# Moving VectorE's work behind a pointwise product: low weights one slot sooner, sums of y spread out, parts of the second half's y sooner

## The chip, the core and the metric

The kernel runs on one core of a Trainium2 chip. The core has a matrix engine (TensorE, PE in the profile), three engines for element-wise work (VectorE or DVE, ScalarE or ACT, GpSimd or POOL) and a queue engine (SyncE, SP) that issues most transfers. The metric is the device time of one execution in microseconds (us). Three runs of the kernel before gave 811.04, 811.59 and 811.87 us; their median is 811.59 us.

## What is computed

One decoder layer on 512 tokens and 2048 channels. After an RMS norm, one wide product makes seven pieces of 1024 columns: value, gate and output gate of a convolution module, q, k, v, and the gate of attention. The convolution half (mixer A) ends in a pointwise projection, the attention half (mixer B) in a gated mixture of three dilated patterns. Both halves meet in the output product.

```
u = silu(layer_norm(causal_depthwise_conv(a_val * sigmoid(a_glu))))
y_a = (u @ conv_pw_w + conv_pw_b) * silu(a_gate)
y_b = dilated_attention_mixture(rms(q), rms(k), v) * silu(b_gate)
out = x + concat(y_a, y_b) @ w_out
```

## The kernel before

Most products are exact to about float32 by being made of float16 pairs. A tile is scaled by a power of two, rounded to float16 (the high part, written by ACT), and the rest is kept as a second float16 tile (the low part, written by DVE as source times scale less high part). `tri` (line 447) then does three matmuls, lines 449, 450 and 451. The scale comes from `bound` (line 215): ACT sums the squares of each piece (`row_squares`, line 213, an ACTIVATE into `junk` with an accumulator), PE adds the columns of sums over partitions by a small matmul with ones (line 225), DVE reduces the result, POOL takes an inverse root (lines 227 and 191), and DVE rounds it to a power of two and inverts it.

Weights come in units of 4 x 128 rows by 512 columns. For a plain unit, `split_hi` (line 326, ACT, tile `wh`) and `split_lo` (line 334, DVE, tile `wl`) make the parts of the next unit while the current one is multiplied. A plain unit is 8 slots; a slot holds 6 matmuls of 512 columns.

All engines run in program order, and the program order is written by hand. `after(n, fn)` (line 143) puts a piece of work n slots ahead in a calendar; tables of numbers at lines 56 to 81 say how far. What is due in a slot is issued before the matmuls of that slot. An instruction that stands late in DVE's order therefore waits for all of DVE's work ahead of it, whatever its own inputs do.

The tail of the program runs as follows. One unit of the output product's group `wb` 0 takes the first half of y_b; then come the pointwise product `pw` (two groups of two units), one unit of `wb` 3 and one of `wc` 0 (they take parts of y_b), and last the four groups `wa` in `seven_products` (line 1097). These replace eight block products by seven, and so need sums of blocks of weights and of blocks of y:

- The evacuation of `pw` (line 929) multiplies by the gate of mixer A. It is the DVE instruction that writes `gate` or `ag` from `ps_l`, four for each group. `put_y` (line 683) has ACT square the result for the bound of all of y (`yab`), and after the second group's four pieces `y_sums` (line 708) forms the block sums: two subtractions at once (`ysum<-ag`, 128x256) and two dependent operations a slot later (`ysum<-gate,ysum`).
- `bound("yab", ...)` gives the scale `yas`. `y_parts` (line 782) then splits sixteen pieces of y (line 748 on ACT, line 749 on DVE).
- The second half of y_b (`b1`) has a scale of its own, `yb1s`. `b_parts` (line 764) splits its four pieces with `plain` (lines 761 and 762) for the unit `wc` 0, and its sums by `y_sums` and `block`. The first half (`b0`) is treated alike, earlier, from line 1393.
- Sums of weight blocks are made in place, partly by DVE and partly by accumulating transfers that POOL issues (line 1038). `both_scales` (line 1084) forms, on POOL, the scales of a `wa` group: `esc`, `nesc` and the joined scales `wjs` (lines 1093 and 1094), which ACT needs for the parts `wsc` and `wsd`.

Of the kernel before, what the change touches and what calls it, by code (L numbers as in the profile page):

```python
# [59 lines left out]
SHIFT_FROM = 3  # L60
SHIFT_STEP = 5
LN_STEPS = [4, 1, 2, 2, 4, 4, 1, 1]
B0_AT = -11
YB = [0, 1, 4, -2, -1, 2]
B_STEPS = [-5, 2, 19, 6]
B1_STEPS = [3, 12, 28, 6]
Y_STEPS = [3, 1]
IN_HI = [-5, -5, -5, -5, -5, -4, -4]
IN_ADD = {('s1', 0): -8, ('s1', 1): -7, ('s2', 0): -1, ('s2', 1): 1, ('s3', 0): 13, ('s3', 1): 11, ('s4', 0): 8, ('s4', 1): 9}
IN_OUT = [4, 8, 16, 9, 12, 16, 20, 24, 24, 25, 25, 27, 28, 29]  # L70
NORM_7 = {'q': [1, 5, 6, 8], 'k': [3, 7, 9, 10]}
NORM = {'q': [3, 8, 8, 10, 5], 'k': [3, 7, 9, 13, 5]}
NORM_K0 = [3, 1, 10, 11, 13, 2]
WA_ADD = [{'s1': (4,), 's4': (1,), 's2': (-2,), 's3': (-8,)}, {'s1': (8, 9, 14), 's4': (2, 3, 8), 's2': (-2, -1, 4), 's3': (-13, -12, -12)}, {'s1': (8, 9, 12), 's4': (2, 3, 8), 's2': (-2, -1, 4), 's3': (-16, -15, -16)}, {'s1': (5, 6), 's4': (0, 2), 's2': (-3, -2), 's3': (-16, -15)}]
WA_PARTS = [{'a11': (-29,), 'a22': (-27,), 'a12': (-1,), 's3': (1,), 's2': (4,), 's1': (7,), 's4': (9,)}, {'a11': (-8, -7, -3), 'a22': (-4, -3, 2), 'a12': (-2, 2, 5), 's3': (4, 5, 10), 's2': (8, 9, 14), 's1': (11, 12, 17), 's4': (15, 16, 21)}, {'a11': (-7, -7, -2), 'a22': (-4, -3, 2), 'a12': (-1, 0, 5), 's3': (4, 5, 10), 's2': (8, 9, 14), 's1': (11, 12, 17), 's4': (15, 16, 21)}, {'a11': (-5, -5), 'a22': (-4, -3), 'a12': (-2, -1), 's3': (0, 1), 's2': (4, 5), 's1': (7, 8), 's4': (10, 11)}]
WA_OUT = [1, 4, 1, 5, 5, 6, 6]
MEASURE = 16
# [1 line left out]
SPLIT_AT = [0, 3]  # L79
# [28 lines left out]
def layer(ctx: ExitStack, tc: tile.TileContext, xt, w1, w2, w3, g_in, conv_w, conv_b,  # L108
# [34 lines left out]
    def after(n, fn):  # L143

        calendar.setdefault(clock[0] + max(n, 1), []).append(fn)
# [180 lines left out]
    def split_hi(i):  # L326
        if i < n_plain:
            parts[i] = [part_pool.tile([P, KU, S], F16, name=n, tag="part") for n in ("wh", "wl")]
            A.activation(parts[i][0], raw[i], AF.Copy, scale=wscale[units[i][3:]][0])  # L329

    def of_next(i):
        return units[min(i + 4, len(units) - 1)][3:]

    def split_lo(i):
        if i < n_plain:
            wh, wl = parts[i]
            V.scalar_tensor_tensor(wl, raw.pop(i), wscale[units[i][3:]][0], wh, op0=OP.mult, op1=OP.subtract)
            load(i + RING)
            after(MEASURE_AT[of_next(i) not in SEVEN], lambda: measure(i + RING))
# [337 lines left out]
    yf = {"a": {}, "b0": {}, "b1": {}}  # L677
# [5 lines left out]
    def put_y(part, i, y):  # L683

        at = i + {"b0": 0, "a": 4, "b1": 12}[part]
        if not ysum:
            ysum.append(small.tile([P, 16], BF16, name="ysum", bufs=1))
        row_squares(y, ysum[0][:, at:at + 1], S, evac_scale(("pw", 0)) if part == "a" else 1.0)
        yf[part][i] = y
        if part != "a" and len(yf[part]) == 4:  # L690
            n = at - 3

            def done(s, v):
                scales["y" + part] = s, v
                if part == "b1":
                    b1_parts()

            after(YB[0], lambda: bound("y" + part, ysum[0][:, n:n + 4], done, TOP - 1, YB[1:3]))
        if part == "a" and i >= 4:
            after(1 + 4 * (i == 7), lambda: y_sums("", yf["a"], i - 4, i))  # L700
        summed.add(at)
        if len(summed) == 16:
            after(YB[3], lambda: bound("yab", ysum[0], y_parts, TOP - 1, YB[4:]))

# [3 lines left out]
    def y_sums(c, y, k, below):  # L708

        b11, b12 = (y[k][:, f:f + H] for f in (0, H))  # L710
        b21, b22 = (y[below][:, f:f + H] for f in (0, H))
        if not c and k < 2:
            t = att.tile([P, 2, S], F32, name="ysum2", tag="att")
            t12, t34 = t[:, 0], t[:, 1]
        else:
            t12, t34 = slot("ysum"), slot("ysum")
        t1, t2, t3, t4 = t12[:, :H], t12[:, H:], t34[:, :H], t34[:, H:]
        V.tensor_sub(t1, b11, b12)
        V.tensor_sub(t3, b12, b22)

        def rest():
            V.tensor_add(t2, b22, t1)
            V.tensor_sub(t4, b21, t2)

        after(1, rest)
        for name, t in (("b11", b11), ("b2", y[below]), ("t12", t12), ("t34", t34)):
            if name[0] == "t" or not c:
                yt[name + c, k] = t
# [35 lines left out]
    def b_parts(part):  # L764
        y = dict(yf[part])
        s = scales["y" + part][0]
        c = "d" if part == "b0" else "c"
        o = B_STEPS if part == "b0" else B1_STEPS
        for k in range(4):
# [12 lines left out]
    def y_parts(s, v):  # L782
# [6 lines left out]
        for name in ("b11", "t34", "b2", "t12"):  # L789
            for k in range(4):  # L790
                n += 1
                after(max(n - Y_STEPS[0], n // Y_STEPS[1]), lambda name=name, k=k: block(name, k, sa))

# [220 lines left out]
    def seven_parts(g):  # L1014
# [62 lines left out]
        for name, at in WA_PARTS[g].items():  # L1077
            for c, n in zip(kinds, at):
                plan += [(n, name + c, hi), (n + 1, name + c, lo)]
        adds = [(n, name + c, add) for name, at in WA_ADD[g].items() for c, n in zip(kinds, at)]  # L1080
        plan = [(n, lambda name=name, fn=fn: fn(name)) for n, name, fn in plan + adds]
# [310 lines left out]

    calendar.setdefault(8 * of_group["wb", 0][0] + B0_AT, []).append(b0_parts)
    for n, fn in seven_parts(0):
        if n < 0:
            calendar.setdefault(BEGIN[0] + n, []).append(fn)
    for i in range(n_plain):
        kind, g = group = units[i][3:]
        if group in SEVEN:
            if i == of_group[group][0]:  # L1400
                plan = ahead.pop(i) + later
                later = []
                n_next = i + 4
                if units[n_next][3:] in SEVEN:
                    ahead[n_next] = input_products(n_next)
                    plan += [(n + 28, fn) for n, fn in ahead[n_next] if n < 0]
                else:
                    plan = [(24, lambda: split_hi(n_next)), (25, lambda: split_lo(n_next))] + plan
                for n in range(28):
                    clock[0] = 8 * i + n + n // 7  # L1410
                    for fn in due_now():
                        fn()
                    first = [fn for k, fn in plan if k == n]
                    for fn in first[:]:
                        if fn.__name__ != "matmuls":
                            fn()
                    run_conv()
                    for fn in first:
                        if fn.__name__ == "matmuls":
                            fn()  # L1420
                later = [(n - 28, fn) for n, fn in plan if n >= 28]
                if units[n_next][3:] not in SEVEN:
                    for n, fn in later:
                        after(8 * n_next + n - clock[0], fn)
                    later = []
                if kind == "k":
                    attention(g)
            continue
        exact = i < n_exact
        if exact:  # L1430
            order = [(None, None)] * 8
        else:
            order = [(m, hf) for m in range(4) for hf in range(2)]
            extra = [[] for _ in range(8)]
            if i + 1 < len(units) and units[i + 1][3:] in SEVEN:
                ahead[i + 1] = input_products(i + 1)
                for n, fn in ahead[i + 1]:
                    if n < 0:
                        extra[max(n, -8)].append(fn)
            else:  # L1440
                extra[SPLIT_AT[0]].append(lambda: split_hi(i + 1))
                extra[SPLIT_AT[1]].append(lambda: split_lo(i + 1))
            if i + 1 < len(units) and units[i + 1][3] == "wb":
                for m in range(2):
                    extra[4 * m].append(lambda m=m: fetch_res(2 * units[i + 1][4] + m))
            if units[i + 1][3] in ("wb", "wc"):
                extra[3].append(lambda: evac_scale(units[i + 1][3:]))
            if units[i + 1][3:] == ("pw", 0) and kind != "pw":
                extra[3].append(pw_bias)
        if kind == "pw":  # L1450
            need = KU * units[i][2] + KU - 1
            while need not in u16:
                next(convolution)
        for n, (m, hf) in enumerate(order):
            clock[0] = 8 * i + n
            if exact:
                extra = {n: startup(clock[0])}
            due = due_now()
            for fn in extra[n] + due if exact or kind in ("wb", "wc") else due + extra[n]:
                fn()  # L1460
            run_conv()
            done = exact_matmuls(clock[0]) if exact else slot_matmuls(i, m, hf)
            if done:
                done()
        if kind == "k" and i == of_group[group][-1]:
            attention(g)
# [71 lines left out]
```

## Time and profile before

| what | value |
|---|---|
| median of three runs | 811.59 us (811.04 to 811.87) |
| the profiled execution | 811.37 us |
| span of its instructions | 809.6 us |
| granted clock of PE | 1.000 |
| busy DVE / ACT / POOL | 718.5 / 571.5 / 162.3 us |
| HBM read | 88.56 MB |

The profile was taken on one execution. Its times count from the first instruction; the 1.8 us between the span and the execution's own time lie outside the instructions. In a timeline a row gives start, duration, engine, line, operation, output and inputs, and in brackets how long the engine had been idle and what released it. DVE's instructions all have line 103, the helper that records them. A plain DVE instruction of 512 columns is shown with about 0.74 us and the next starts 0.66 us after it, so an engine's rows may overlap slightly. The profile prints the tiles `y16` as `y`.

### The profile page before, as it was taken

Reading aid. Unit: us, or ns where it says so; the run is one execution under the profiler, and the core shown is the slowest. Engines: PE = TensorE matmul, PEld = TensorE weight load, DVE = VectorE, ACT = ScalarE, POOL = GpSimd, SP = SyncE. Lnnn points to the kernel's source line nnn. Section 1 sums busy time; section 2 is a strip of 40 time slices with the busy share of each in tenths; the row PEclk is TensorE's granted clock in tenths of the full one; section 3 lists DMA queues with packets and bytes.
Section 4 is the critical chain, followed back from the end, with each engine's and each line's share of the span. In section 5 each row is a group of like instructions: output and inputs, shape, how many; then the busy total and the mean of one; then the engine's idle time right before and its main releaser. Section 6 shows DMA issues by size and latency. Waiting matters only on the chain.

```text
span 809.6 us, 13885 instructions
## 1 busy us (share of the span) xinstructions
PE 801.9 (99%) x5448; PEld 518.5 (64%) x5448; DVE 718.5 (89%) x1208; ACT 571.5 (71%) x800; POOL 162.3 (20%) x165
## 2 busy tenths in 40 slices
PE   9999999999999999999999999999999999999998
PEld 6887745888888854444444444444544444888887
DVE  6768899899999989999899999899699679998784
ACT  6667775677878697757849458496799868667530
POOL 0002021213535101104113010110230012423310
PEclk9999999999999999999999999999999999999999
DMA  9853253685979946352863825327282646898551
GB/s 339 337 232 104 105 145 98 123 261 94 299 160 272 224 150 169 105 147 82 175 170 102 182 94 157 117 66 165 95 199 75 165 161 157 208 223 233 106 117 53
DMA packets 88097, 130.87 MB, mean 162 GB/s; under 512 B 62688, under 2 KB 67040, under 8 KB 78816
## 3 DMA queue, kind: packets, MB, share of 16 engines
q1 hardware_dynamic: 80544, 107.37, 43.2%
q0 software_dynamic: 7200, 22.55, 15.5%
q8 instruction: 42, 0.69, 0.3%
q14 instruction: 23, 0.19, 0.1%
q10 hardware_dynamic: 288, 0.07, 0.0%
HBM read 88.56 MB, written 4.19 MB: 115 GB/s over the span
## 4 chain that ended last, share of the span: by engine, by line
PE 92%; DVE 5%; POOL 1%; ACT 1%; issue 1%; DMA 0%; SPq 0%; DVEq 0%; POOLq 0%; ACTq 0%
PE ps_l L449 24%; PE ps_l L450 24%; PE ps_l L451 24%; PE ps_l L978 11%; PE ps_s L824 2%; PE ps_o L865 2%; PE ps_s L449 2%; PE ps_s L451 2%; PE ps_s L450 2%; DVE res L103 1%; DVE y L103 1%; DVE ysum L103 1%; DVE ws L103 0%; POOL wf L1038 0%; DMA x<-xt_dram 0%
## 5 line engine op out<-in xcount | busy, mean ns | idle before, releaser
L103 DVE SCALAR_TENSOR_TENSOR cv<-u,cw,cv 128x511 f32<-128x511 f32 (+14 forms) x240 | 162.2, 727 | 2.7 <-ACT cv L614 2.7
L213 ACT ACTIVATE junk<-wf 128x2048 uint8<-128x2048 f32 x68 | 129.1, 1899 | 8.8 <-DMA wf<-w_dram 8.7
L449 PE MATMUL ps_l<-x,wh 128*128 128x512 f16 x320 | 121.3, 379 | 0.0
L451 PE MATMUL ps_l<-x,wl 128*128 128x512 f16 x320 | 121.3, 379 | 0.0
L450 PE MATMUL ps_l<-x,wh 128*128 128x512 f16 x320 | 121.3, 379 | 0.0
L103 DVE SCALAR_TENSOR_TENSOR ws<-wf,ws 128x1024 f16<-128x1024 f32 x84 | 107.2, 1278 | 8.0 <-ACT ws L1216 6.8
L329 ACT ACTIVATE wh<-wf,ws 128x2048 f16<-128x2048 f32 x39 | 77.7, 1993 | 25.5 <-PE ps_l L450 21.5
L103 DVE SCALAR_TENSOR_TENSOR wl<-wf,ws,wh 128x2048 f16<-128x2048 f32 x39 | 91.4, 2344 | 3.1 <-ACT wh L329 2.9
L449 PEld LDWEIGHTS <-wh 128*128 128x128 f16 x432 | 42.3, 98 | 54.1 <-issue 5.0
L451 PEld LDWEIGHTS <-wl 128*128 128x128 f16 x432 | 42.2, 98 | 52.0 <-issue 1.1
L450 PEld LDWEIGHTS <-wh 128*128 128x128 f16 x432 | 42.2, 98 | 48.4 <-issue 0.3
L449 PE MATMUL ps_l<-wh,x 128*128 128x512 f16 x192 | 72.8, 379 | 0.0
L451 PE MATMUL ps_l<-wh,x 128*128 128x512 f16 x192 | 72.8, 379 | 0.0
L450 PE MATMUL ps_l<-wl,x 128*128 128x512 f16 x192 | 72.8, 379 | 0.0
L978 PE MATMUL ps_l<-xr,wr 128*128 128x512 f32 x288 | 69.6, 397 | 0.2 <-ACT xr L367 0.2
L227 POOL TENSOR_SCALAR ws<-ws 128x1 f32<-128x1 f32 x20 | 18.7, 937 | 248.0 <-DVE ws L103 247.5
L1216 ACT ACTIVATE ws<-wf,ws 128x1024 f16<-128x1024 f32 x56 | 62.3, 1136 | 1.0 <-ACT ws L1216 0.3
L978 PEld LDWEIGHTS ps_l<-xr,wr 128*128 128x128 f32 x288 | 53.9, 188 | 13.8 <-ACT xr L367 1.1
L191 POOL TENSOR_TENSOR ss<-ss,half 128x8 f32<-128x8 f32 x16 | 35.4, 2216 | 92.4 <-DVE ss L103 92.4
L449 PE MATMUL ps_l<-ws,tx 128*128 128x256 f16 x192 | 52.3, 273 | 0.0
L451 PE MATMUL ps_l<-ws,tx 128*128 128x256 f16 x192 | 52.3, 273 | 0.0
L450 PE MATMUL ps_l<-ws,tx 128*128 128x256 f16 x192 | 52.3, 273 | 0.0
(287 smaller groups left out, 1935.8 us busy)
## 6 DMA issues: line engine op xcount, KB each, us to landing
wf<-w_dram SPq DMA_DIRECT2D x72, 1024.0 KB, 5.4
wf<-wf POOLq DMA_DIRECT2D x36, 512.0 KB, 6.0
x<-xt_dram SPq DMA_DIRECT2D x16, 256.0 KB, 6.6
res<-xt_dram SPq DMA_DIRECT2D x8, 512.0 KB, 6.2
out_dram<-res SPq DMA_DIRECT2D x15, 256.0 KB, 3.7
wf<-w_dram SPq DMA_DIRECT2D x7, 512.0 KB, 7.2
wf<-wf POOLq DMA_DIRECT2D x12, 256.0 KB, 6.8
wf<-w_dram SPq DMA_DIRECT2D x2, 256.0 KB, 3.6
```

Of the source, the lines that this page charges most:

```text
L103: return getattr(self.engine, name)(out, src, *args, **kw)
L191: G.tensor_tensor(ap, ap, half.to_broadcast(list(ap.shape)), op=OP.pow)
L213: A.activation(junk[:, :n], src, AF.Square, scale=scale, accum_out=acc)
L227: G.tensor_scalar(scale, scale, 1e-24 if name == "u" else 1e-30, 2.0 ** (-2 * top), op0=OP.max, op1=OP.mult)
L329: A.activation(parts[i][0], raw[i], AF.Copy, scale=wscale[units[i][3:]][0])
L449: T.matmul(ps, ah, bh, start=first, stop=False, skip_group_check=more)
L450: T.matmul(ps, ah, bl, start=False, stop=False, skip_group_check=more)
L451: T.matmul(ps, al, bh, start=False, stop=last, skip_group_check=more)
L824: T.matmul(ps[i, a], qk["q", hf][p4 // 2][rows, p4 % 2, q, i * P:w], qk["k", hf][p4 // 2][rows, p4 % 2, k, :w], start=n == 0, stop=n == 2)
L865: T.matmul(po[rows, i * P:(i + 1) * P], vs[hf][j // 2][:, j % 2, 2 * p4 + a, vp * DH:(vp + 1) * DH], got["t", a][:, pp * (ALL // P) + FROM ...
L978: T.matmul(banks[group, m], wt[:, a, m * P:(m + 1) * P], xk[b], start=k == 0 and a == b == 0, stop=k == KC - 1 and a == 1)
L1216: A.activation(t[:, 0], block(name, pair), AF.Copy, scale=wscale[group][0])
```

## The change

Eight edits, all of them to the order; no instruction is added or removed on any engine.

- `SPLIT_PW`: while the second `pw` group is multiplied, the high parts of the next unit's weights keep slot 0, and the low parts go to slot 2 in place of 3.
- `Y_SUMS`: the block sums of mixer A's y are issued 2, 1, 2 and 1 slots after the four evacuations of that group, in place of 1, 1, 1 and 5.
- `YB`: the rounding of the scale `yab` waits one slot more.
- `Y_STEPS`: its first number goes from 3 to 5. It stands in `max(n - Y_STEPS[0], n // Y_STEPS[1])` with a second number of 1, which is n either way.
- `B1_STEPS`: the sums of the second half of y_b come 3 slots sooner.
- `B0_AT` and `B_STEPS`: the four parts of the first half of y_b come 2 slots sooner, the sums behind them by up to one slot.
- `WA_ADD`, first group: one accumulating transfer (`s2`) stands 2 slots sooner in POOL's order.
- `WA_ADD`, second group: three accumulating transfers (`s3`) stand 3 slots later, behind `both_scales` of that group.

```diff
-B0_AT = -11
-YB = [0, 1, 4, -2, -1, 2]
-B_STEPS = [-5, 2, 19, 6]
-B1_STEPS = [3, 12, 28, 6]
-Y_STEPS = [3, 1]
+B0_AT = -13
+YB = [0, 1, 4, -2, -1, 3]
+B_STEPS = [-5, 3, 20, 7]
+B1_STEPS = [3, 9, 28, 6]
+Y_STEPS = [5, 1]
+Y_SUMS = [2, 1, 2, 1]
+SPLIT_PW = [0, 2]
...
-WA_ADD = [{'s1': (4,), 's4': (1,), 's2': (-2,), 's3': (-8,)}, {'s1': (8, 9, 14), 's4': (2, 3, 8), 's2': (-2, -1, 4), 's3': (-13, -12, -12)}, {'s1': (8, 9, 12), 's4': (2, 3, 8), 's2': (-2, -1, 4), 's3': (-16, -15, -16)}, {'s1': (5, 6), 's4': (0, 2), 's2': (-3, -2), 's3': (-16, -15)}]
+WA_ADD = [{'s1': (4,), 's4': (1,), 's2': (-4,), 's3': (-8,)}, {'s1': (8, 9, 14), 's4': (2, 3, 8), 's2': (-2, -1, 4), 's3': (-10, -9, -9)}, {'s1': (8, 9, 12), 's4': (2, 3, 8), 's2': (-2, -1, 4), 's3': (-16, -15, -16)}, {'s1': (5, 6), 's4': (0, 2), 's2': (-3, -2), 's3': (-16, -15)}]
...
         if part == "a" and i >= 4:
-            after(1 + 4 * (i == 7), lambda: y_sums("", yf["a"], i - 4, i))
+            after(Y_SUMS[i - 4], lambda: y_sums("", yf["a"], i - 4, i))
...
-                extra[SPLIT_AT[0]].append(lambda: split_hi(i + 1))
-                extra[SPLIT_AT[1]].append(lambda: split_lo(i + 1))
+                at_hi, at_lo = SPLIT_PW if kind == "pw" and g else SPLIT_AT
+                extra[at_hi].append(lambda: split_hi(i + 1))
+                extra[at_lo].append(lambda: split_lo(i + 1))
```

What these numbers do to the order is seen in the instructions themselves. The changed file has two lines more at its top, so its line numbers are 2 higher (3 higher from line 1444 on). In the names, `gate<-ps_l` is an evacuation of `pw`, `ysum` a block sum, `wl` low weights, `y_` a part of y.

The first place is DVE's order around the last two evacuations of `pw`, before the change:

```order
L103 SCALAR_TENSOR_TENSOR gate<-ps_l,pwb,gate 128x512
L103 TENSOR_SCALAR yb1s<-yb1s 128x1
L103 RECIPROCAL yb1i<-yb1s 128x1
L103 TENSOR_TENSOR ysum<-ag_5348 128x256
L103 TENSOR_TENSOR ysum<-ag_5348,gate 128x256
L103 TENSOR_TENSOR ysum<-gate,ysum 128x256 x2
L103 SCALAR_TENSOR_TENSOR gate<-ps_l,pwb,gate 128x512
L103 SCALAR_TENSOR_TENSOR y_6912<-gate,yb1s,y_6912 128x512
L103 TENSOR_REDUCE yabs<-ps_s 128x1
L103 SCALAR_TENSOR_TENSOR res<-ps_l,esc,res 128x512
```

and with it:

```order
L105 TENSOR_TENSOR ysum<-ag_5348,gate 128x256
L105 SCALAR_TENSOR_TENSOR gate<-ps_l,pwb,gate 128x512
L105 TENSOR_TENSOR ysum<-gate,ysum 128x256 x2
L105 SCALAR_TENSOR_TENSOR y_6912<-gate,yb1s,y_6912 128x512
L105 TENSOR_TENSOR ysum<-ag_5348 128x256
L105 TENSOR_TENSOR ysum<-ag_5348,gate 128x256
L105 TENSOR_REDUCE ws<-ps_s 128x1
L105 TENSOR_TENSOR ysum<-gate,ysum 128x256 x2
L105 TENSOR_REDUCE yabs<-ps_s 128x1
L105 SCALAR_TENSOR_TENSOR res<-ps_l,esc,res 128x512
```

The last evacuation moved ahead of the dependent half of the third piece's sums, and the fourth piece's sums, which stood ten rows further down, moved up between it and the reduction of `yabs`. Ahead of this place, `wl` moved from behind the first piece's sums to ahead of them.

The second place is DVE's order around the fourth part of the second half of y_b (`y_7027` in both), before:

```order
L103 SCALAR_TENSOR_TENSOR y_7005<-ag_5348,yas,y_7005 128x256
L103 SCALAR_TENSOR_TENSOR res<-ps_l,esc,res 128x512
L103 SCALAR_TENSOR_TENSOR y_7027<-gate,yb1s,y_7027 128x512
L103 SCALAR_TENSOR_TENSOR y_7031<-ysum_6849,yas,y_7031 128x2x256
L103 SCALAR_TENSOR_TENSOR y_7042<-ysum_6879,yas,y_7042 128x2x256
L103 SCALAR_TENSOR_TENSOR res<-ps_l,esc,res 128x512
L103 TENSOR_TENSOR ysum<-gate 128x256 x2
```

and with the change:

```order
L105 TENSOR_TENSOR ysum<-gate 128x256 x2
L105 SCALAR_TENSOR_TENSOR y_7017<-ag_5348,yas,y_7017 128x256
L105 SCALAR_TENSOR_TENSOR res<-ps_l,esc,res 128x512
L105 SCALAR_TENSOR_TENSOR y_7027<-gate,yb1s,y_7027 128x512
L105 TENSOR_TENSOR ysum<-gate,ysum 128x256 x2
L105 SCALAR_TENSOR_TENSOR y_7017<-ag_5348,yas,y_7017 128x256
```

Two sums of the second half (`ysum<-gate`) moved ahead of `y_7027`, and the last part of mixer A's blocks (`ag_5348`) went behind it.

The third place is POOL's order from the scale `yab` on, before:

```order
L191 TENSOR_TENSOR yabs<-yabs,half 128x1
L462 TENSOR_TENSOR esc<-wi,yabi 128x1
L1089 TENSOR_SCALAR nesc<-esc 128x1
L227 TENSOR_SCALAR ws<-ws 128x1
L191 TENSOR_TENSOR ws<-ws,half 128x1
L462 TENSOR_TENSOR esc<-wi,yb1i 128x1
L1038 DMA wf<-wf 128x1024 x4
L1038 DMA wf<-wf 128x512 x2
L462 TENSOR_TENSOR esc<-wi,yabi 128x1
L1089 TENSOR_SCALAR nesc<-esc 128x1
L1093 TENSOR_TENSOR wjs<-ws,yabs 128x1
```

and with the change:

```order
L193 TENSOR_TENSOR yabs<-yabs,half 128x1
L464 TENSOR_TENSOR esc<-wi,yb1i 128x1
L464 TENSOR_TENSOR esc<-wi,yabi 128x1
L1091 TENSOR_SCALAR nesc<-esc 128x1
L1040 DMA wf<-wf 128x1024 x3
L464 TENSOR_TENSOR esc<-wi,yabi 128x1
L1091 TENSOR_SCALAR nesc<-esc 128x1
L1095 TENSOR_TENSOR wjs<-ws,yabs 128x1
L1096 TENSOR_TENSOR wjs<-wjs,yb1i 128x1
```

The last three of the six accumulating transfers (one of 128x1024, two of 128x512) moved behind the scales `esc`, `nesc` and `wjs` of the second `wa` group. The first `esc` and `nesc` of `yab` now stand directly ahead of the transfers.

## Prediction

> **What bounds the kernel now.** I read the page first, then PE's waits in the timeline, then the share of each engine around them.
>
> ```profile
> PE 801.9 (99%) x5448; PEld 518.5 (64%) x5448; DVE 718.5 (89%) x1208; ACT 571.5 (71%) x800; POOL 162.3 (20%) x165
> PE 92%; DVE 5%; POOL 1%; ACT 1%; issue 1%; DMA 0%; SPq 0%; DVEq 0%; POOLq 0%; ACTq 0%
> ```
>
> PE is busy nearly always, and the chain that ended last is PE's for 92%. The change takes no matmul away, so all it can win is time in which PE stands still. PE's timeline shows its waits in the tail (duration first, then in brackets the wait and what ended it):
>
> ```profile
> 665.07 0.17 PE L225 MATMUL ps_s<-ysum,ones 128*128 128x16 bf16 x1 [1.61 <-ACT junk L213]
> ...
> 677.36 0.38 PE L450 MATMUL ps_l<-y,wh 128*128 128x512 f16 x1 [0.85 <-DVE y L103]
> ...
> 702.03 0.28 PE L451 MATMUL ps_s<-y,ws 128*128 128x256 f16 x1 [0.37 <-DVE ws L103]
> ...
> 709.12 0.28 PE L451 MATMUL ps_l<-y,wsd 128*128 128x256 f16 x1 [0.37 <-DVE wsd L103]
> ...
> 713.61 0.27 PE L450 MATMUL ps_l<-y,wsc 128*128 128x256 f16 x1 [0.17 <-DVE y L103]
> ```
>
> Five waits, 1.61 + 0.85 + 0.37 + 0.37 + 0.17 = 3.4 us by these rows. After 713.61 PE waits for nothing the profile shows, so whatever PE is ahead by there is the gain. Four of the five are released by DVE, and the first by ACT on DVE's behalf. DVE's load in this stretch:
>
> ```profile
> 653.00:684.00 31.00, 28.54 (x134) 12.79 (x134) 28.40 (x58) 23.14 (x36) 8.96 (x12) 1.00 0.50 152
> 684.00:714.00 30.00, 29.09 (x256) 24.70 (x255) 29.09 (x40) 20.18 (x25) 11.54 (x14) 1.00 0.81 191
> ```
>
> (Columns: stretch, its length, then busy time of PE, PE's loads, DVE, ACT, POOL.) From 653 to 714 DVE is busy for 57.5 of 61 us. It is the pacer there, and PE gains only where DVE gets ahead.
>
> **Step A, the sum at 665.07.** DVE and ACT ahead of it:
>
> ```profile
> 662.57 0.88 DVE L103 TENSOR_TENSOR ysum<-gate,ysum 128x256 f32<-128x256 f32 x2
> 663.37 0.74 DVE L103 SCALAR_TENSOR_TENSOR gate<-ps_l,pwb,gate 128x512 f32<-128x512 f32 x1
> 664.06 0.75 DVE L103 SCALAR_TENSOR_TENSOR y<-gate,yb1s,y 128x512 f16<-128x512 f32 x1
> 665.28 0.17 DVE L103 TENSOR_REDUCE yabs<-ps_s 128x1 f32<-128x16 f32 x1 [0.47 <-PE ps_s L225]
> 666.65 0.75 DVE L103 SCALAR_TENSOR_TENSOR res<-ps_l,esc,res 128x512 f32<-128x512 f32 x1 [1.20 <-PE ps_s L225]
> ```
>
> ```profile
> 660.56 1.91 ACT L213 ACTIVATE junk<-wf 128x2048 uint8<-128x2048 f32 x1
> ```
>
> ```profile
> 664.21 0.72 ACT L213 ACTIVATE junk<-gate,esc 128x512 uint8<-128x512 f32 x1 [0.18 <-DVE gate L103]
> 664.83 0.19 ACT L213 ACTIVATION_READ_ACCUMULATOR junk<-gate,esc 128x1 bf16 x1
> ```
>
> The last evacuation waits in DVE's order behind the dependent pair of sums, 663.37 - 662.57 = 0.80 us. In the new order the pair stands behind it. The evacuation ends at 663.31, ACT's squares follow 0.10 later as now, and PE's sum moves from 665.07 to 664.27. ACT is free for that: the 1.91 us of weight squares at 660.56, which kept the third piece waiting, stand one piece earlier in its new order. PE reaches this matmul when it does now, so its wait shrinks from 1.61 to 0.81. Gain so far **0.80**.
>
> The low weights `wl` and the first sums only change places ahead of 661, which gives nothing by itself. It does put the reduction of `yb1s` behind `wl`:
>
> ```profile
> 655.75 0.15 DVE L103 TENSOR_REDUCE yb1s<-ps_s 128x1 f32<-128x4 f32 x1
> ```
>
> ```profile
> 661.66 0.14 DVE L103 TENSOR_SCALAR yb1s<-yb1s 128x1 int32<-128x1 int32 x1
> ```
>
> Some 2.3 later it stands at 658.0, and POOL has 3.6 us left for its two small operations before DVE rounds the result at 661.66. At the 2.21 us of POOL's slow row in step C they would be 0.8 late; I take 0.
>
> More comes of it on DVE. Its two idle pieces, 0.47 and 1.20, lie between the last evacuation and the first `res`. The new order fills them: pair 0.80, `y` 0.66, the fourth piece's sums 1.47, a reduction 0.1 start from 663.23 and end at 666.3, by when the matmuls that `res` needs, 0.80 sooner, are done at 665.85. DVE is then 0.47 + 1.20 = **1.67 ahead**.
>
> The price is that `yas` comes later. It now stands behind `res`, `y` and `wl`:
>
> ```profile
> 668.37 2.34 DVE L103 SCALAR_TENSOR_TENSOR wl<-wf,ws,wh 128x2048 f16<-128x2048 f32 x1
> ```
>
> That is 666.35 + 0.66 + 0.66 + 2.26, and 0.25 for the three small ones: 670.2, against 667.7 now. The parts that need it belong to the `wa` products, which begin after the unit that PE is still at in its row of 677.36; DVE makes the first of them at 671.96 (row in step B), over 5 us before. That lead is the cover, and I cost the step at nothing on PE; up to 2.5 less 1.67 us would be due if it failed. POOL is taken up in step C.
>
> **Step B, the part of y at 677.36.**
>
> ```profile
> 676.56 0.74 DVE L103 SCALAR_TENSOR_TENSOR y<-gate,yb1s,y 128x512 f16<-128x512 f32 x1
> ```
>
> ```profile
> 679.21 0.75 DVE L103 TENSOR_TENSOR ysum<-gate 128x256 f32<-128x256 f32 x2
> ```
>
> ```profile
> 671.96 0.47 DVE L103 SCALAR_TENSOR_TENSOR y<-ag,yas,y 128x256 f16<-128x256 f32 x1
> ```
>
> Of DVE's 1.67, this instruction loses the pair of sums put ahead of it (0.67 to the next start) and wins the part of `ag` put behind it (0.39): 1.67 - 0.28 = **1.39**. PE's matmul moves from 677.36 to 675.97. The wait is then 0.85 - (1.39 - 0.80) = 0.26, since PE itself was 0.80 sooner.
>
> **Step C, the waits from 702 on.** By 690 both orders hold the same set of work, so DVE is its full 1.67 ahead. One more idle piece lies on the way:
>
> ```profile
> 699.37 0.75 DVE L103 SCALAR_TENSOR_TENSOR wsc<-wf,wjs,wsc 128x512 f16<-128x512 f32 x1 [0.84 <-ACT wsc L1051]
> ```
>
> ```profile
> 698.61 0.72 ACT L1051 ACTIVATE wsc<-wf,wjs 128x512 f16<-128x512 f32 x1 [2.41 <-POOL wjs L1094]
> ```
>
> ```profile
> 668.58 2.21 POOL L1089 TENSOR_SCALAR nesc<-esc 128x1 f32<-128x1 f32 x1
> ...
> 672.02 0.94 POOL L1038 DMA_DIRECT2D wf<-wf  x1
> 683.67 0.87 POOL L1038 DMA_DIRECT2D wf<-wf  x1 [10.72 <-issue]
> 690.06 3.56 POOL L1038 DMA_DIRECT2D wf<-wf  x4 [5.52 <-DVE ysum L103]
> 692.28 2.69 POOL L462 TENSOR_TENSOR esc<-wi,yabi 128x1 f32<-128x1 f32 x1
> ...
> 697.46 1.12 POOL L1094 TENSOR_TENSOR wjs<-wjs,yb1i 128x1 f32<-128x1 f32 x1
> ```
>
> Four transfers were issued from 690.06, then came the scales until 698.58. Three of the four now stand behind the scales. The one left waited for DVE; 1.67 sooner it goes out at 688.4, takes 0.9, and the scales start at 689.3 in place of 692.28. With unchanged durations `wjs` ends at 695.6 and ACT's `wsc` at 696.4. DVE wants it at 699.37 - 0.84 - 1.67 = 696.86, so the 0.84 goes too, and DVE is 2.51 ahead. If the transfer can't leave before 690.06, because the one ahead of it in the chain lands no sooner, the scales end 1.4 sooner only, and DVE is 699.37 - 1.4 = 697.97, some 1.4 ahead. I take the first: POOL's row names DVE, not a transfer, as what ended its wait. What goes the other way is that the first transfer, issued at 672.02, now follows `esc` and `nesc`, which need `yas` at 670.2. Two POOL operations take between next to nothing and 2 x 2.21, so it leaves between 670.2 and 674.6; at 1.12 each, as in the row of `wjs`, at 672.4, and I take that: 0.4 later than now.
>
> PE in step C: it comes in 1.39 ahead, and drops the waits of 0.37, 0.37 and 0.17, each released by a DVE row that is 2.51 ahead. That makes 2.30, which is under DVE's 2.51.
>
> `nesc`, 2.21 us for one column, begins inside `wl` at 668.37 and ends at 670.79, 0.08 behind it. The Trainium skill, page "SBUF — State Buffer", section "SBUF: two separate sides", has a rule that speaks against this change: a DVE instruction with two SBUF inputs and a POOL instruction that reads SBUF exclude each other for the whole of the one that came first. The trace agrees with it in this row. By that rule a DVE without idle time stretches POOL's scales; stretched by more than the 0.5 us that `wsc` has to spare they would leave part of the 0.84, and the sum would be that of the first rival, 809.7, against 809.1.
>
> **The three transfers put later** leave about 6 us later, at 696 to 698. By the trace:
>
> ```profile
> DMA to landing us min/median/max: 4.5/6.4/11.1
> ```
>
> (wf from 668 to 720.) They would land by 709 at the latest. Their first follower on POOL went out at 708.02 before, and PE's waits after 713.61 don't show them. Cost: nothing; 0 to 1 us if the slowest landing meets the follower, which is then no later than now.
>
> **First half of y_b, 574 to 597.**
>
> ```profile
> 574.00:597.00 23.00, 23.00 (x116) 11.32 (x116) 19.27 (x44) 21.60 (x38) 6.45 (x5) 1.00 0.41 109
> ```
>
> Four parts (4 x 0.66) and a pair of sums (0.67) pass ahead of two small `hl` pieces and one `cv`: those come 3.3 us later, the last two `hl`, which end the tile, as now. PE has 23.00 of 23.00 there, and DVE 3.7 us free. Cost 0 on PE, at most 3.3 if that cover failed; I take 0. `Y_STEPS` changes no value.
>
> **Sum.** 0.80 + (1.39 - 0.80) + 0.37 + 0.37 + 0.17 = 2.30. The profiled execution took 811.37 (its span 809.6 and 1.8 around it): 811.37 - 2.30 = 809.07, told as **809.1**. The median shown is 0.2 above that execution, so from it the same sum gives 809.3. A measurement of this kernel can tell about 0.2%, 1.6 us, from no change.
>
> **Rivals.**
> 1. *POOL's chain keeps its place.* The idle 0.84 stays in part, DVE is 1.4 to 1.67 ahead at 713, and the gain is that: 809.7 to 810.0. For it: the late `yas`, the late first transfer, the busier DVE. Against it: 3 us less queue on POOL. Chance 0.20, half of it over 0.2%.
> 2. *The sums are only moved.* The last evacuation was not what PE waited for, or the filled idle time returns further down as another DVE wait before 713: a gain of 0 to 1, 810.4 to 811.4. Against it: the wait at 665.07 ends 0.05 behind ACT's accumulator, and that 0.10 behind DVE. Chance 0.13.
> 3. *Slower, by the chain of accumulating transfers.* The first, at 672.02, lets out the second at 683.67, and that one the third at 690.06, with all scales of the second `wa` group and `wsc` behind it. The scales would have to start after 692.28, the third transfer to leave after 691.4. The second takes at least 4.5 (the shortest landing), so it lands at 688.2 or later; the case decides from the point where the first is 3.2 us later than now. Each us past that is lost whole: 6 us late gives 811.37 + 2.8 = 814.2. Against it: at most 2.6 of it comes from the later issue, so the transfer, already the longest of its kind at about 11, would have to take some 12 with all of that and 14 with the 0.4 I expect, and 1.6 more to be told from no change. Chance 0.07.
>
> **How the numbers follow.** The forecast has 0.60. Faster: 0.60 + 0.10 = 0.70; within 0.2%: 0.10 + 0.13 = 0.23; slower 0.07. The range runs from 808.5 (the whole 2.51 and 0.3 of scatter) to 810.9, over rival 1 and half of rival 2.
>
> **What would show it.** PE's wait at line 225 near 0.8 us in place of 1.6; DVE without idle time from the last evacuation of `pw` to the first `wsc`; the wait for `y` near 0.3; the waits for `ws` and `wsd` gone; POOL's `wjs` ending near 695.6. A new wait of PE on a transfer or on `wsc` after 690, or one in 574 to 653, would prove me wrong.

## The result, and the profile after

| | median, us | runs | lowest to highest | ratio to before, 95% interval |
|---|---|---|---|---|
| before | 811.38 | 10 | 811.04 to 811.87 | |
| the change | 809.03 | 10 | 808.29 to 810.59 | 0.9973 [0.9963, 0.9983] |

The change is faster by 2.35 us, and the median lies 0.07 from the forecast. Its runs spread over 2.3 us where those of before spread over 0.8, and the execution that was profiled, 810.59 us (span 808.8), is the slowest of the ten. So this profile shows two things: what the change wins, and how part of it is lost again.

TensorE's load and the chain that ended last, from the page of the changed kernel:

```profile
PE 802.1 (99%) x5448; PEld 518.9 (64%) x5448; DVE 718.1 (89%) x1208; ACT 571.4 (71%) x800; POOL 161.2 (20%) x165
...
PE 88%; DVE 7%; DMA 4%; issue 1%; POOL 0%; ACT 0%; SPq 0%; POOLq 0%; ACTq 0%; DVEq 0%
```

DMA had 0% of the chain before and has 4% now. Where PE still waits from 640 us on, in the waits of PE (in total, times, longest):

```profile
PE ps_l L451 <- ACT wsd L1053: 1.0, 1, 1.0
PE ps_s L227 <- ACT junk L215: 0.8, 1, 0.8
PE ps_l L453 <- DVE wsd L105: 0.4, 1, 0.4
```

The wait for `junk` is that of step A, halved as reckoned. The waits of 677, 702, 709 and 713 are gone. Two are new, and the timeline of PE puts them at 745, where before had none:

```profile
744.57 0.28 PE L451 MATMUL ps_l<-y,wsd 128*128 128x256 f16 x1 [1.02 <-ACT wsd L1053]
...
745.36 0.28 PE L453 MATMUL ps_l<-y,wsd 128*128 128x256 f16 x1 [0.40 <-DVE wsd L105]
```

By stretches (columns as in the prediction), the changed kernel:

```profile
653.00:684.00 31.00, 30.14 (x150) 13.66 (x146) 29.78 (x62) 24.41 (x38) 7.18 (x12) 1.00 0.52 155
684.00:714.00 30.00, 29.94 (x274) 26.58 (x273) 29.96 (x38) 20.84 (x27) 12.58 (x13) 1.00 0.75 178
714.00:750.00 36.00, 34.58 (x318) 30.50 (x316) 28.86 (x43) 23.04 (x29) 11.01 (x17) 1.00 0.90 243
```

and before in the last of them:

```profile
714.00:750.00 36.00, 36.00 (x333) 32.27 (x332) 32.06 (x46) 25.29 (x33) 11.09 (x17) 1.00 0.91 236
```

PE is busy 1.60 us more up to 684 and 0.85 more up to 714, and then 1.42 less. DVE is busy all of the second stretch (29.96 of 30.00), as step C said.

To follow PE exactly, one needs a rod that leaves the start of the program out. I take the time from PE's small sum at 655.50 (it lies ahead of everything that changes PE's time) to PE's last matmul. Before:

```profile
655.50 0.17 PE L225 MATMUL ps_s<-ysum,ones 128*128 128x4 bf16 x1
...
806.22 0.22 PE L451 MATMUL ps_s<-y,wsc 128*128 128x128 f16 x1
```

and with the change:

```profile
655.76 0.17 PE L227 MATMUL ps_s<-ysum,ones 128*128 128x4 bf16 x1
...
805.42 0.22 PE L453 MATMUL ps_s<-y,wsc 128*128 128x128 f16 x1
```

That is 150.72 against 149.66, a gain of 1.06 in this execution. With each matmul's start set against that of the same matmul before, counted in the same way, PE's **lead** is 0.82 at 667 us, 1.62 at 679, 2.16 at 703, 2.71 at 711 and **2.81 from 715 to 743**; at 745 it loses 1.76. So the prediction's steps gave more than its 2.30, and what it had costed at nothing took some back.

The chain of the changed kernel shows the way of the loss (start, duration, what):

```profile
710.02 7.70 DMA wf<-wf
...
718.79 7.35 DMA wf<-wf
...
730.75 0.67 DVE wsc L105
731.44 10.38 DMA wf<-w_dram
741.90 0.21 ACT junk L215
...
743.90 0.62 ACT wsd L1053
744.55 0.76 DVE wsd L105
745.36 0.28 PE ps_l L453
```

Two accumulating transfers, one after the other, then `wsc`, whose end frees a weight block; its refill takes 10.38 us. ACT's squares of that block wait for it, and in ACT's order they stand ahead of the `wsd` that PE needs. Why this chain is late is told by POOL's queue. The changed kernel:

```profile
695.83 1.12 POOL L1096 TENSOR_TENSOR wjs<-wjs,yb0i 128x1 f32<-128x1 f32 x1
696.88 2.73 POOL L1040 DMA_DIRECT2D wf<-wf  x3
706.99 0.86 POOL L1040 DMA_DIRECT2D wf<-wf  x1 [7.38 <-DVE wsd L105]
710.02 0.86 POOL L1040 DMA_DIRECT2D wf<-wf  x1 [2.16 <-DVE ws L105]
716.35 0.86 POOL L1040 DMA_DIRECT2D wf<-wf  x1 [5.47 <-DVE wsc L105]
```

The three transfers put later leave at 696.88, and the view of `wf` for them gives

```profile
DMA to landing us min/median/max: 9.6/11.9/13.2
```

so the first lands at 706.5, and the next transfer leaves 0.5 later; the second lands at 709.5, and the follower at 710.02 leaves 0.6 later. The program makes them wait: `seven_products` forms its sums in place, and a follower adds the block that a late transfer has written (`SUMS` and `PLACE`, lines 1011 and 1012 of the changed kernel). The follower at 710.02 is no later than before (710.03; counted from the rod it is 0.26 sooner), but PE is 2.81 further on.

### The profile page after: what moved, and what is told of

Read it like the earlier page. It is cut to its first block, busy times and chain, and to the rows that moved or that the text cites. A ratio compares the mean times of both kernels' runs of the same rounds, so it can differ in the third digit from the quotient of the medians.

```text
span 808.8 us, 13884 instructions
## 1 busy us (share of the span) xinstructions
PE 802.1 (99%) x5448; PEld 518.9 (64%) x5448; DVE 718.1 (89%) x1208; ACT 571.4 (71%) x800; POOL 161.2 (20%) x165
## 4 chain that ended last, share of the span: by engine, by line
PE 88%; DVE 7%; DMA 4%; issue 1%; POOL 0%; ACT 0%; SPq 0%; POOLq 0%; ACTq 0%; DVEq 0%
PE ps_l L451 23%; PE ps_l L453 23%; PE ps_l L452 23%; PE ps_l L980 11%; DMA wf<-wf 2%; PE ps_s L826 2%; PE ps_o L867 2%; DVE y L105 2%; DVE res L105 1%; DMA wf<-w_dram 1%; PE ps_s L451 1%; PE ps_s L453 1%; PE ps_s L452 1%; DVE ws L105 1%; DVE ysum L105 1%
```

## The experiments

Two theories stood after this profile. **T**: the three late transfers hold up their followers, and with them the refill and the `wsd` of 745. **L**: the chain of the second group starts at its own clock whatever these transfers do, and PE only ran out of slack. Beside them the parts of the change were taken back one by one. Leads and losses are by the rod above; "before" is the kernel before, timed in the same session (medians 811.41 to 811.55).

**e1, transfers back.**

```diff
-'s3': (-10, -9, -9)
+'s3': (-13, -12, -12)
```

> The kernel after, with the three accumulating transfers of s3 back at their slots of before (-13, -12, -12), so that they leave ahead of the scales on POOL again. Main theory (step C is real, and what is given back near 745 us comes from the second group's own chain of transfers and weight load, which the change never moved): the scales end near 698.5 us instead of 696.95, VectorE has 0.8 us of idle ahead of its first wsc again, TensorE stands 1.6 to 1.9 us ahead of before at 714 us instead of 2.56, and that fits into the slack at 745, so nothing is given back there: 809.5 to 809.9 us, and a spread of the runs under 1.2 us. Rival T (the three late transfers are what delays the second group's transfers, and the scales' place is worth little): the waits at 745 us go and the time is 808.3 to 808.7, faster than the change. Rival N (the move of s3 does nothing in either direction): 809.0 with the change's spread of 2.3 us.

Measured: 809.32 us (809.14 to 810.11, 10 runs), ratio 0.9973 [0.9964, 0.9982]. Lead 1.90, all of it kept. DVE waits for its first `wsc` again, by exactly the piece that step C had removed:

```profile
697.81 0.75 DVE L105 SCALAR_TENSOR_TENSOR wsc<-wf,wjs,wsc 128x512 f16<-128x512 f32 x1 [0.84 <-ACT wsc L1053]
```

As expected, a little under the range; but as T too would have no loss here, the loss doesn't separate the two. What T added, that the scales' place is worth little, is wrong: the lead is 0.91 smaller.

**e5, transfers and scales both early.** `s3` as in e1, and

```diff
-            if n == LENGTH[g] - 10 and g < 3:
+            if n == (1 if g == 0 else LENGTH[g] - 10) and g < 3:
```

> The kernel after, with the three transfers of s3 at their slots of before and the scales of the second group issued ahead of everything else of that point, three slots sooner, so that scales and transfers are both early. Rival T (late transfers cause the give-back): TensorE is 2.5 us or more ahead at 714 us, no wait on wsd near 745 us, 808.2 to 808.6 us with a spread under 1.2 us. Main theory (the chain that begins with the transfer at 710.0 us and ends in the weight load at 731.4 us starts at the same clock whatever the three transfers do): TensorE 2.5 us ahead at 714 us, waits of 0.5 to 1.8 us together near 745 us remain, 808.7 to 809.3 us, the same as the change.

Measured: 808.59 us (808.24 to 808.61, 5 runs), 0.9962 [0.9949, 0.9974]. Lead 2.81, loss 0. The rod reads 147.91:

```profile
655.51 0.17 PE L227 MATMUL ps_s<-ysum,ones 128*128 128x4 bf16 x1
...
803.42 0.22 PE L453 MATMUL ps_s<-y,wsc 128*128 128x128 f16 x1
```

POOL's queue shows why:

```profile
705.23 0.87 POOL L1040 DMA_DIRECT2D wf<-wf  x1 [13.27 <-DVE ws L105]
707.21 0.87 POOL L1040 DMA_DIRECT2D wf<-wf  x1 [1.12 <-DVE wsc L105]
711.89 0.87 POOL L1040 DMA_DIRECT2D wf<-wf  x1 [3.81 <-DVE wsd L105]
```

With the transfers away by 692 they land by 699.6, long before the followers, and these move with DVE and PE: 707.21 is 710.03 less 2.82. The profile of the changed kernel names DVE's `ws` as what released the follower at 710.02; in e5 that follower leaves at 707.21, ahead of the start of that `ws` (708.16), so it was not waiting for it. In all five profiles with the transfers late (the changed kernel twice, e6, e3 and e2) the first two followers leave 0.5 and 0.6 us after the first two landings. T holds, and L, my main theory in that expectation, falls.

**e6, squares behind `wsd`.** The late transfers stay; only the squares of the block refilled from 731.44 go one slot later.

```diff
-                after(9, lambda: measure(i + RING))
+                after(10 if g == 1 and i == of[0] else 9, lambda: measure(i + RING))
```

> The kernel after, with ScalarE's squares of one weight block (the one whose load leaves at 731.44 us) one slot later, so that they stand behind the first half of wsd in ScalarE's queue and no longer ahead of it; nothing else of the order near 745 us changes. Main theory (TensorE's new waits at 744.57 and 745.36 us are ScalarE waiting for that load with wsd queued behind it): both waits go, TensorE keeps its lead of 2.5 us through 745, and the time is 808.2 to 808.6 us with a spread under 1.2 us. Rival (wsd itself is late, because its block wf comes late out of the accumulating transfers or VectorE reaches it late): the wait on wsd stays at 0.8 us or more under the name of VectorE or a transfer, and the time stays at 808.9 to 809.3.

Measured: 808.78 us (808.44 to 809.14, 5 runs), 0.9965 [0.9951, 0.9978]. Lead 2.82, loss 0. ACT's timeline of this kernel:

```profile
739.20 0.71 ACT L1053 ACTIVATE wsc<-wf,wjs 128x512 f16<-128x512 f32 x1
739.81 0.71 ACT L1053 ACTIVATE wsd<-wf,wjs 128x512 f16<-128x512 f32 x1
740.42 1.90 ACT L215 ACTIVATE junk<-wf 128x2048 uint8<-128x2048 f32 x1
```

The follower on POOL left at 710.03, as late as in the changed kernel, and ACT could start `wsd` at 739.81, ahead of the refill's landing at 740.2 (issued at 730.73, 9.5 us). So `wsd` itself does not need the refill, and it was the squares in ACT's queue that passed its lateness on. How much the edit saves this profile doesn't show: its refill came 1.6 us sooner than in the first profile of the change, and with the squares ahead of `wsd` I estimate a loss of under 0.2.

**e3, sums and low weights back.** `Y_SUMS = [1, 1, 1, 5]`, `SPLIT_PW = [0, 3]`.

> The kernel after, with the sums of y and the low weights behind the pointwise product back at their slots of before (1, 1, 1, 5 and 3). Main theory (steps A and B come from these two): TensorE's wait at 665 us on junk is 1.6 us again instead of 0.8, VectorE has its 1.2 to 1.7 us of idle between 660 and 670 us back, what is left is step C's 0.84 us at most: 810.5 to 811.0 us. Rival (the sums were only moved, and the time came from the earlier yb1 and the scales): 809.0 to 809.4 us.

Measured: 811.29 us (810.49 to 813.0, 11 runs), 0.9999 [0.9991, 1.0008]. PE's wait at 665 is 1.6 again, the one at 677 is 1.3, the lead at 715 is 0.74, and 1.50 are lost at 745: the gain of the whole change goes, and the time is 0.3 over the range expected, which had no loss at 745 in it. The loss comes at a lead under 1 us, and the follower left at 711.54, 1.8 us later than before by the rod, which speaks for T as well. To see the parts without it, the next three start from e5.

**The changed kernel again.**

> The changed kernel once more, unedited. In its first profile the follower of the three late transfers left POOL at the moment the second of them landed, and TensorE lost 1.8 us of its lead near 745 us. Theory (what is given back depends on how long the three late transfers happen to take): the lead at 714 us is 2.8 us again to within 0.05, what is lost at 745 us is another amount than before, anywhere from 0 to 2 us, and the ten runs spread over more than 1 us, between 808.2 and 810.7, with a median of 808.6 to 809.4. Rival (a fixed loss of 1.8 us): 810.0 or more in every run, which its first runs already speak against.

Measured: 808.67 us (808.55 to 808.85, 6 runs), 0.9968 [0.9956, 0.9981]. Lead 2.80, loss 0.03 in place of 1.76. The transfers left and landed as before (9.6 to 13.2 us), the follower left at 709.77, but the refill left 0.85 us sooner by the rod and took 9.5 us in place of 10.4, and ACT's squares waited for it less:

```profile
739.86 1.91 ACT L215 ACTIVATE junk<-wf 128x2048 uint8<-128x2048 f32 x1 [0.32 <-DMA wf<-w_dram]
```

The loss differs from run to run as expected, but these six runs spread over 0.3 us, not over more than 1, and the reason expected is wrong: the three late transfers took the same time in both profiles. They set when the chain behind them can start; what differed came further down, in that chain and in the refill.

**e7, low weights back** (on e5): `SPLIT_PW = [0, 3]`.

> The kernel with scales and transfers early (e5), with only the low weights behind the pointwise product back at slot 3. Theory S (the spread sums are what brings the last pointwise evacuation forward, the low weights only swap places with smaller work): TensorE's wait at 664 us stays at 0.8 us, its lead on before stays 1.6 us at 679 and 2.8 us at 715, and the time stays at 808.2 to 808.8 us. Rival W (the low weights a slot sooner bring step A): the wait is 1.6 us again, and the time 809.2 to 809.7.

Measured: 808.72 us (808.41 to 808.94, 5 runs), 0.9968 [0.9956, 0.9981]. Lead 2.80. The low weights a slot sooner are worth nothing.

**e8, sums back** (on e5): `Y_SUMS = [1, 1, 1, 5]`.

> The kernel with scales and transfers early (e5), with only the sums of y back at slots 1, 1, 1 and 5. Theory S (the sums bring step A): two sums of 0.3 us each stand ahead of the last pointwise evacuation again, TensorE's wait at 664 us is 1.4 to 1.6 us, and VectorE has idle time back behind it that the sums filled: 809.2 to 810.4 us. Rival W (it was the low weights): 808.2 to 808.8.

Measured: 810.44 us (810.31 to 811.2, 11 runs), 0.9991 [0.9982, 1.0]. Lead 0.73. PE's timeline:

```profile
665.63 0.17 PE L227 MATMUL ps_s<-ysum,ones 128*128 128x16 bf16 x1 [1.61 <-ACT junk L215]
...
678.37 0.38 PE L452 MATMUL ps_l<-y,wh 128*128 128x512 f16 x1 [1.33 <-DVE y L105]
```

and DVE's waits from 660 to 714:

```profile
DVE res L105 <- PE ps_l L453: 1.2, 1, 1.2
DVE yabs L105 <- PE ps_s L227: 0.4, 1, 0.4
```

The two idle pieces of step A (1.2 and 0.4) are back, and the cost is 2.08 us of lead, a little over the range expected.

**e9, parts of y back** (on e5): `B0_AT`, `B_STEPS`, `B1_STEPS`, `YB` and `Y_STEPS` as before.

> The kernel with scales and transfers early (e5), with the steps of both halves of y (its y_b0 and y_b1 parts and their bounds) back at their numbers of before; sums, low weights, scales and transfers stay. Theory (the earlier parts of y_b1 are what VectorE does in the idle time of step A, and y_b0 ahead of 600 us is worth nothing): nothing changes ahead of 650 us, the wait at 664 us stays 0.8, but the wait for y at 677 us comes back at 0.4 to 0.9 us and VectorE is later by up to that for step C: 808.9 to 809.9 us. Rival (the order of the y parts is worth nothing, VectorE is held by the sum of its work): 808.2 to 808.8.

Measured: 809.51 us (809.02 to 809.82, 11 runs), 0.9975 [0.9966, 0.9984]. Lead 2.04: nothing ahead of 650, 0.82 at 667 as in e5, then 0.50 lost at 677 and 0.27 from 703 to 715. The size is as expected, but the theory's reason is not what DVE's timeline shows. In e5 DVE has no idle time from 655 to 715; in e9 it stands idle in front of the rounding of `yab`, which `YB` had moved one slot on:

```profile
668.17 0.15 DVE L105 TENSOR_SCALAR yabs<-yabs 128x1 int32<-128x1 int32 x1 [0.66 <-POOL yabs L193]
```

From start to start that is 0.75 us, nearly all of the 0.77 lost by 715. At 677 the old order of the second half gives 0.28 of it back, as step B had reckoned. So by the rows it is the one slot of `YB` that counts, and nothing in them speaks for a gain by the earlier parts of y_b; no run took `YB` back alone.

**e10, the sum of squares a slot later** (on e5): the fifth number of `YB` is 2.

> The kernel with scales and transfers early (e5), with TensorE's column sums of the squares of y one slot later (the fifth number of YB 2 instead of -1), so that twelve matmuls stand ahead of them and the last wait of that stretch, 0.81 us at 664 us, is covered; VectorE's order changes in one place only (the reduction of these sums behind one evacuation instead of ahead of it). Theory D (VectorE, which has no idle time from 662.8 us to its first wsc, holds TensorE behind 670 us): the wait at 664 goes, TensorE is 1.6 us ahead of before at 667, but waits for y, ws or wsd come back between 677 and 714 us, its lead at 715 is 2.8 us again, and the time is 808.2 to 808.8 us. Rival P (TensorE's own waits were the bound): lead 3.6 us at 715, 807.6 to 808.0 us.

Measured: 809.25 us (808.99 to 809.71, 8 runs), 0.9974 [0.9964, 0.9984]. The wait at 664 goes, and PE is 1.77 ahead at 667; then

```profile
676.42 0.38 PE L452 MATMUL ps_l<-y,wh 128*128 128x512 f16 x1 [1.56 <-DVE y L105]
```

The lead falls to 1.06 at 679 and is 2.25 at 715. DVE is the bound behind 670, as theory D said; that the one reduction put later would cost 0.56 on top was not foreseen, and the time is above the range. It is the wait of e9 again: POOL gets `yabs` later, its second operation lasts as long as `wl` beside it, and DVE waits for the result:

```profile
668.01 2.51 POOL L193 TENSOR_TENSOR yabs<-yabs,half 128x1 f32<-128x1 f32 x1
```

```profile
670.55 0.15 DVE L105 TENSOR_SCALAR yabs<-yabs 128x1 int32<-128x1 int32 x1 [0.45 <-POOL yabs L193]
```

**e2 and e11, step C alone on the kernel before.** e2 has only the new `s3`, e11 only the early scales of e5.

> The kernel before, with only the three transfers of s3 put later (-10, -9, -9), which moves them from ahead of the second group's scales to behind them on POOL. Theory (step C stands on its own and so does its price): TensorE gains 0.9 to 1.2 us between 700 and 715 us, the three transfers leave at 698 to 700 us and land late, the follower leaves POOL near 711.5 instead of 710.03, and 0 to 1.5 us are given back near 745 us: 810.3 to 812.0 us, spread over 1 us. Rival (the follower's lateness costs nothing while TensorE is less than 1.5 us ahead): 810.2 to 810.7 us, nothing lost at 745.

> The kernel before, with only the second group's scales issued three slots sooner and so ahead of the three transfers of s3, which stay where they were. Theory (the scales' place on POOL is what step C gains by, without a price when the transfers stay early): a lead of 0.9 to 1.2 us at 715 us, nothing lost at 745: 810.2 to 810.7 us with a spread under 1.2 us. Rival (VectorE's idle ahead of wsc is hidden by other waits of the tail, so that the scales help only together with steps A and B): 811.2 to 811.6 us, no lead at 715.

Measured: e2 810.88 us (810.12 to 815.4, 12 runs), 0.9992 [0.9983, 1.0001]; e11 810.33 us (810.13 to 811.7, 11 runs), 0.9988 [0.9979, 0.9997]. Both have a lead of 0.92 at 715. e11 keeps it; its runs spread over 1.6 us, more than the 1.2 expected. e2's profiled execution, its slowest, turns it into 3.44 behind: its squares waited for their refill 2.58 us,

```profile
745.01 1.91 ACT L213 ACTIVATE junk<-wf 128x2048 uint8<-128x2048 f32 x1 [2.58 <-DMA wf<-w_dram]
...
746.92 0.71 ACT L1051 ACTIVATE wsd<-wf,wjs 128x512 f16<-128x512 f32 x1
```

and PE 1.95 for the `wsd` behind them and 0.40 more for its low part, which from start to start cost 2.69. The other 1.67 of the 4.36 lost is not a wait: from 749.5 to 752.9 the granted clock of PE was half (third figure from the end of the row, 0.51 for the stretch), and matmuls of 256 columns started 0.21 apart in place of 0.11.

```profile
749.50:753.00 3.50, 3.50 (x20) 2.50 (x18) 3.50 (x7) 3.50 (x6) 0.90 (x2) 0.51 0.37 105
```

No other profile here shows a lower clock in the tail before its last matmul. The medians are not told apart, and e2's profile is of its slowest run, 4.5 us over the median, so its loss is no typical one. But the pair differs only in where the transfers stand beside equally useful scales, and the loss at 745 is with the late ones, whose follower left 1.6 us later than before by the rod. At so small a lead PE had not run out of slack, which speaks against L.

Over all profiles: with the transfers early (e1, e5, e7 to e11) nothing is lost at 745 in seven of seven. With them late and the squares ahead of `wsd`, four profiles lost 1.76, 0.03, 1.50 and 2.69 there (e2's halved clock left out).

## Why the prediction was right, and where it was not

**What bounds the kernel.** Right: every gain came where DVE got ahead, and the profile shows no wait of PE from 679 to 743.

**Step A** said 0.80; the lead is 0.82, and the wait is 0.81 as told. The last evacuation now stands ahead of its neighbour's dependent sums, and the fourth piece's sums fill DVE's idle time:

```profile
662.82 0.74 DVE L105 SCALAR_TENSOR_TENSOR gate<-ps_l,pwb,gate 128x512 f32<-128x512 f32 x1
663.48 0.88 DVE L105 TENSOR_TENSOR ysum<-gate,ysum 128x256 f32<-128x256 f32 x2
...
666.47 0.17 DVE L105 TENSOR_REDUCE yabs<-ps_s 128x1 f32<-128x16 f32 x1
666.55 0.74 DVE L105 SCALAR_TENSOR_TENSOR res<-ps_l,esc,res 128x512 f32<-128x512 f32 x1
```

e8 shows that the sums do it, e7 that the low weights do nothing. `yas` ends at 670.5, against 670.2 told, and only POOL waited for it, 0.29. What the step booked as a price, the later `yas`, is by e9 what keeps DVE from waiting for POOL.

**Step B** said a wait of 0.26 left, a gain of 0.59. The lead grew by 0.80 and 0.05 is left. DVE was 1.61 ahead by then, not 1.39 (its row of 676.56 now starts at 675.20, 1.36 sooner, in a profile whose rod stands 0.26 later). The term that was off is the 1.67. A bracket counts idle time from the shown end of the row before, but rows overlap: before, `y` at 664.06 and the reduction at 665.28 start 1.22 apart, and now, with nothing to wait for, `y` and the instruction behind it start 0.66 apart. From start to start the idle pieces were 0.56 and 1.29, so 1.85, and 1.85 - 0.28 = 1.57.

**Step C** said 0.91, by the three waits in brackets; the lead grew by 1.19 (0.54, 0.55, 0.10). The first two were read too small in the same way: matmuls of 256 columns start 0.11 apart and are shown with 0.27, so a bracket of 0.37 costs 0.54. (So do the two new waits at 745: 1.02 and 0.40 in brackets, 1.76 of lead.) The last gain is what DVE allowed: DVE's idle 0.84 was 0.92 from start to start, and 1.85 + 0.92 = 2.77 is close to the 2.81 at which PE's lead stops. Alone on the kernel before step C is 0.92. The scales moved as reckoned (`esc` from 689.25, the first `wsc` of DVE at 696.81 without a wait), and e1 brings back exactly the 0.84 in brackets, 0.91 of lead. So A, B and C together are **2.81, not 2.30**. Rivals 1 and 2 fall with that: POOL's chain did not keep its place, and e8 shows that the sums were not only moved.

**The rule weighed in step C.** The six scale operations take 7.7 us in the changed kernel (689.25 to 696.95), 6.7 before (692.28 to 698.99) and 2.5 in e5:

```profile
683.17 0.51 POOL L464 TENSOR_TENSOR esc<-wi,yabi 128x1 f32<-128x1 f32 x1
683.77 0.61 POOL L1091 TENSOR_SCALAR nesc<-esc 128x1 f32<-128x1 f32 x1
684.35 0.66 POOL L1095 TENSOR_TENSOR wjs<-ws,yabs 128x1 f32<-128x1 f32 x1
685.09 0.19 POOL L1096 TENSOR_TENSOR wjs<-wjs,yb1i 128x1 f32<-128x1 f32 x1
```

There DVE runs instructions of 0.66 us beside them, and at 685 an evacuation from PSUM; in the changed kernel, from 693.22, three of 1.2 us, and POOL's operations last 1.1 to 1.2. This agrees with the Trainium skill, "SBUF — State Buffer", section "SBUF: two separate sides". The stretch was there, 1.0 us, but the joined scale that `wsc` waits for ended at 694.55, early enough.

**The three transfers put later** is the step that failed: "Cost: nothing; 0 to 1 us if the slowest landing meets the follower, which is then no later than now." The landing times were taken from before, 4.5 to 11.1 us, and gave 709 at the latest; they were 9.6 to 13.2, and 711 for the last. And the test was put wrongly. The follower was indeed no later than before, by 0.01, but a step that puts PE 2.8 us ahead needs everything behind it 2.8 us sooner, or slack of that size. The price is 0 to 1.8 us in the profiles of the changed kernel and 2.7 in that of e2. PE's waits after 713.61, which I had looked for in before, could not show it: there was none because PE was later.

**The sum** came out at 809.07 against 809.03. That is partly luck: the steps were sized 0.5 too small, because brackets were added up where starts should have been, and the loss left out took about as much. Without the loss the kernel is at 808.59 to 808.78 (e5, e6), which 811.37 - 2.81 = 808.56 gives. The range, 808.5 to 810.9, held the median, though single runs went down to 808.29.

**The first half of y_b** cost nothing, as told: PE's starts, counted from the rod, are the same to 0.01 us from 560 to 663. **Rival 3** did not occur: the chain it feared, from 672 to 690, held (the transfer ahead of the scales left at 688.67). Its mechanism, a late accumulating transfer whose lateness passes on whole, did occur, one group of transfers later.

e5 is the best version found. It has no wait left but the 0.81 of step A, and e10 shows that covering that one loses more. Against the changed kernel it is not told apart by the medians (808.59 against 809.03 and 808.67).

**Open.** Why the late transfers land slowly was not tried. Two weight loads of 1 MB leave within 3 us of them, at 696.9 and 699.4 us, which is an argument only. Nor was it settled why the refill took 9.5 us in one run and 10.4 in another, or why the clock fell in e2's profile.

## What to carry to other kernels

When a change lets the pacing engine run ahead, ask of every transfer behind that place not "is it later than now?" but "is it as much sooner as the engine is?"; a chain that keeps its clock becomes the next wait. When something is moved behind something else on a queue to let that one go first, look for an order that has both early, as e5 does. A wait in brackets understates the time lost wherever rows overlap: take the distance from start to start, less the one without a wait. And a lead that changes from run to run at one place points to transfers: an instruction that waits for a load should not stand, on an in-order engine, ahead of one that PE is about to need.

## What the runs showed of the hardware

- PE's leads repeat to 0.03 us from one kernel and run to the next (2.80 to 2.82 at 715 in the changed kernel, its repeat, e5, e6 and e7); only what hangs on transfers varies.
- The same three accumulating transfers landed 6.8 to 9.0 us after they were issued (behind one more) at 690 us, and 9.6 to 13.2 us at 697 us.
- A one-column operation on POOL took 0.19 us beside a DVE evacuation from PSUM (e5), 1.1 to 1.8 beside DVE's longer operations on SBUF (the changed kernel, from 691.5), and 2.51 beside `wl` (e10).
- In the one profile in which PE waited 1.95 us in the tail (e2) its granted clock was half from 749.5 to 752.9 us, beginning 1.8 us after that wait; waits of up to 1.61 there left it at full. That is one event, and its cause is not shown.
